# A new order for the mixer of a two-layer hybrid decoder trunk, with a new beginning and a new end

## Chip, cores and metric

One core of one Trainium2 chip runs the whole program. The metric is the device time of one execution in microseconds (us); of a kernel the median over several executions counts, and lower is better.

## What is computed

Two layers over 512 tokens of width 1024, everything in float32. In a layer, `x` goes through a SwiGLU half-step, a mixer, and a second SwiGLU half-step:

```python
x = x + 0.5 * swiglu(rms_norm(x, norm_ffn1[l]), ffn1_w_gate[l], ffn1_w_up[l], ffn1_w_down[l])
x = x + hybrid_mixer(rms_norm(x, norm_mix[l]), w_in[l], w_proj_dil[l], w_proj_sb[l], w_out[l], cos, sin)
x = x + 0.5 * swiglu(rms_norm(x, norm_ffn2[l]), ffn2_w_gate[l], ffn2_w_up[l], ffn2_w_down[l])
...
return rms_norm(x, norm_final)
```

The mixer projects its input to queries, keys and values of 16 heads and to two gates of width 1024. Twelve heads form three groups of dilated window attention (with partial rotary, merged over groups by their softmax denominators). Four heads do stick-breaking attention, whose weights for a query are `exp(log_beta + after)`, where `after` is a running sum of `log_sigmoid(-z)` from the right. Then

```python
y = gate_dil * (o_dil @ w_proj_dil) + gate_sb * (o_sb @ w_proj_sb)
return y @ w_out
```

## The kernel before

Activations lie transposed, features on the 128 partitions and 512 tokens along the free axis, as eight tiles `x0` to `x7`. A float32 product is made of three TensorE matmuls on values split into a rounded high part and a remainder (`mm3`, lines 142 to 144). All weights come from one long array in the order in which they are used, in chunks of eight 128x128 blocks. `Weights.fill` loads a chunk and splits a quarter (four blocks, 128x512) at a time: ScalarE casts `whi` (line 76), VectorE subtracts to get `wlo` (line 77). It runs two quarters ahead of use. Whatever order the projections have in the code must be the order in which `_pack_layer` packs the blocks.

`Norm` scales `x` by the gain and splits it (`scale`, lines 173 to 181), sums squares (`square`), and `finish` turns the sum into a reciprocal root per token, as a row `rb` copied from PSUM to SBUF (line 236). In the first half-step squares and scales of the eight tiles are made up front; `feed` does both for a tile as soon as the stage before has written it. `finale` makes the last two blocks of the last half-step by halves of the tokens and multiplies the result by `rb` (line 295) before it is stored.

The mixer runs in this order of code: both V halves (eight banks of PSUM between them, lines 340 to 376), with `norm.finish` after the first weight quarter; then for each of two pairs of stick-breaking heads `qk_pair`, scores and values together (`stick`, lines 447 to 483); then for each of two dilated head sets `s` the rotary `qk_pair`s and scores, with gates in between as `GATES` says (`dil_scores`), the softmax (`dil_softmax`) and the values (`dil_values`); then the sigmoid gates with the two output projections (`apply_gate`, lines 654 to 660), with one gate pair (d = 7) still to be projected, and `w_out`. A stick-breaking score tile takes Abs, Exp and Ln on ScalarE, an add, a reversed scan (line 464) and a subtraction on VectorE, and an Exp on ScalarE.

PSUM banks go by letter: `m`, `t`, `s`, `o`, two buffers each. The code's order is not the engines' order: the framework's scheduler plays the program on a model of the engines and lets later work go ahead of waiting work, within the banks and buffers that are free; each engine then runs its list strictly in that fixed order.

Of the kernel before, what the change touches and what calls it, by code (L numbers as in the profile page):

```python
# [41 lines left out]

class Weights:
# [4 lines left out]
    def __init__(self, nc, raw, split, hold, w):  # L50
        self.nc, self.raw, self.split, self.hold, self.w = nc, raw, split, hold, w
        self.nq = w.shape[0] * (CB // QB)
        self.pos = 0
        self.ready = {}
        self.done = 0
        self.chunk = None

    def fill(self, q):
        nc = self.nc
        while self.done <= q and self.done < self.nq:  # L60
            c, part = divmod(self.done, CB // QB)
            if part == 0:
                self.chunk = self.raw.tile([P, CB * P], F32, name="wraw", tag="wraw")
                step = P if c == 0 else CB * P
                for o in range(0, CB * P, step * QB):
                    e = min(o + step * QB, CB * P)
                    nc.sync.dma_start(self.chunk[:, o:e], self.w[c, :, o:e])
# [8 lines left out]
            nc.scalar.copy(hi, src)  # L76
# [29 lines left out]
def trunk(ctx, tc, xin, win, gains, rope, masks, out, depth):  # L106
# [16 lines left out]

    nc.scalar.preload_act_table_set(SIGM)
    gain = const.tile([P, gains.shape[1]], F32, name="gain")
    nc.sync.dma_start(gain, gains)
    weights = Weights(nc, rawp, splitp, hpool, win)
    xs = []
    for k in range(KD):
# [3 lines left out]
        if k == 0:  # L133
            weights.fill(0)
# [22 lines left out]
    class Norm:  # L157


        def __init__(self, g, table=None):  # L160
# [4 lines left out]
            self.h = [None] * KD  # L165
            self.acc = None
            self.rest = []

        def feed(self, k):
            self.scale(k)  # L170
            self.square(k)

        def scale(self, k):
            x = xs[k]
            gk = gain[:, self.g + k:self.g + k + 1]
            if not self.last:
                hi = hpool.tile([P, T], F32R, name=f"xh{k}", tag=f"xh{k}")
                lo = hpool.tile([P, T], F32R, name=f"xl{k}", tag=f"xl{k}")
                nc.scalar.activation(hi, x, AF.Copy, bias=0.0, scale=gk)
# [36 lines left out]
        def finish(self, j0=0, j1=NT):  # L216
# [20 lines left out]
            self.rt, self.rb = rt, rb  # L237

    def ffn(norm, nxt, first):
        with ExitStack() as st:  # L240
# [6 lines left out]
            for f in range(NF):  # L247
                pg, pu = [bank(b) for b in ("mt", "mt", "oo")[f % 3]]
                project(pg, norm.h)
                project(pu, norm.h)  # L250
                if f == 0:
                    if first:
                        for k in range(KD):
                            norm.square(k)
                    norm.finish_wide(nw, onesr)
# [21 lines left out]
    def finale(st, hs, nxt):  # L277
# [3 lines left out]
        for c0 in range(0, T, HT):  # L281
# [9 lines left out]
            for k in range(0, KD, 2):  # L291
                o = op.tile([P, 2, HT], F32, name="o", tag="o")
                eng = nc.gpsimd if k == 2 else nc.vector
                for i in range(2):
                    eng.tensor_mul(o[:, i], xs[k + i][:, c], nxt.rb[:, :HT])
                nc.sync.dma_start(out[k:k + 2, :, c].rearrange("k p t -> p k t"), o)

    def mixer(norm, nxt):
# [7 lines left out]
        pp = pool(st, "mixp", 8)  # L306
# [33 lines left out]
        pv = []  # L340
        for half in range(2):
            pv.append([bank(b) for b in ("mmtt", "ssoo")[half]])
            for k in range(KD):
                wh, wl = weights.quarter()
                for j in range(NT):
                    c = slice(j * P, (j + 1) * P)
                    ps = pv[half][j]
                    a, b = h[k][0][:, c], h[k][1][:, c]
                    nc.tensor.matmul(ps, a, wh, start=k == 0, stop=False)
                    nc.tensor.matmul(ps, a, wl, start=False, stop=False)  # L350
                    nc.tensor.matmul(ps, b, wh, start=False, stop=k == KD - 1)
                if half == 0 and k == 0:
                    norm.finish()
                    nc.gpsimd.tensor_mul(cr, cr, norm.rb)
                    nc.gpsimd.tensor_mul(sr, sr, norm.rb)

            def split_v(dst, src, sc):
                v = src.rearrange("p (h d) -> p h d", d=HD)
                nc.scalar.activation(dst[:, :, 0, :], v, AF.Copy, bias=0.0, scale=sc)
                nc.vector.scalar_tensor_tensor(dst[:, :, 1, :], v, sc, dst[:, :, 0, :].bitcast(F32),  # L360
                                               ALU.mult, ALU.subtract)

            if half == 0:
                v0, vs = [], []
                for j in range(NT):
                    sc = norm.rt[:, j:j + 1]
                    for lst, nm, off in ((v0, "v0", 0), (vs, "vs", 256)):
                        t = vp.tile([P, 4, 2, HD], F32R, name=f"{nm}_{j}", tag=f"{nm}_{j}")
# [471 lines left out]
```

## Time and profile before

| | |
|---|---|
| median of 3 runs | 2169.5 us (2168.34 to 2170.79) |
| the profiled execution, its own time | 2166.81 us |
| its span, first to last instruction | 2165.0 us |
| TensorE (PE) busy | 2136.6 us, 99% |
| VectorE (DVE) busy | 1209.4 us, 56% |
| ScalarE (ACT) busy | 892.7 us, 41% |
| GpSimd (POOL) busy | 374.4 us, 17% |
| mean granted TensorE clock | 0.996 |

The profile counts a matmul as busy until its modelled end, and matmuls overlap, so a PE that is 99% busy can still issue more slowly than it might. The two mixers lie at 372 to 672 us and 1443 to 1743 us of the span.

### The profile page before, as it was taken

To read this page: it belongs to the slowest core of one execution; us is meant where nothing else is said; L and a number is where in the kernel's file an instruction comes from. 1 tells how busy PE (TensorE), PEld (TensorE's weight loads), DVE (VectorE), ACT (ScalarE), POOL (GpSimd) and SP (SyncE) were. 2 spreads that over 40 slices of the span, in tenths; PEclk is the share of its full clock that TensorE was granted. 3 is DMA by queue.
4 is the path that set the end of the run, shared out by engine and by line. 5 is a ranking of instruction groups with operands and counts; after the bars stand their busy time and mean duration, and the time that the engine had idled before them with its cause. 6 is when DMAs were issued, how large, how long until landed. Compare 5 with 4: busy or idle time off the path is not lost.

```text
span 2165.0 us, 25866 instructions
## 1 busy us (share of the span) xinstructions
PE 2136.6 (99%) x9772; PEld 1764.2 (81%) x9772; DVE 1209.4 (56%) x1896; ACT 892.7 (41%) x1572; POOL 374.4 (17%) x396
## 2 busy tenths in 40 slices
PE   8999999999999999999999999999999999999998
PEld 7888888878887888888888888888788788888887
DVE  7544433589867655443354444336897666444433
ACT  5333323566564433332333333236664544333332
POOL 2222100021412122210022220000223212222100
PEclk9999999999999999999999999999999999999999
DMA  4333333232224233323233333333222233323222
GB/s 153 97 97 98 102 105 125 88 93 87 79 74 129 96 97 98 97 97 98 88 98 97 98 98 107 108 117 94 87 83 78 79 126 98 98 97 97 97 90 86
DMA packets 64621, 212.80 MB, mean 98 GB/s; under 512 B 7408, under 2 KB 9456, under 8 KB 64496
## 3 DMA queue, kind: packets, MB, share of 16 engines
q1 hardware_dynamic: 63920, 210.10, 30.4%
q8 instruction: 76, 1.25, 0.2%
q10 hardware_dynamic: 576, 1.05, 0.2%
q14 instruction: 49, 0.40, 0.1%
HBM read 200.63 MB, written 6.29 MB: 96 GB/s over the span
## 4 chain that ended last, share of the span: by engine, by line
PE 91%; DVE 5%; issue 2%; ACT 1%; POOL 1%; DMA 0%; SPq 0%; DVEq 0%; POOLq 0%; ACTq 0%
PE ps_o L142 14%; PE ps_o L143 14%; PE ps_o L144 14%; PE ps_m L142 9%; PE ps_m L143 9%; PE ps_m L144 9%; PE ps_t L143 5%; PE ps_t L142 5%; PE ps_t L144 5%; DVE wlo L77 1%; DVE sc L464 1%; PE ps_o L620 0%; POOL bn L554 0%; ACT pt L545 0%; PE ps_s L422 0%
## 5 line engine op out<-in xcount | busy, mean ns | idle before, releaser
L77 DVE TENSOR_TENSOR wlo<-wraw,whi 128x512 fp32r<-128x512 f32 x736 | 593.6, 809 | 584.1 <-ACT whi L76 583.5
L76 ACT CAST whi<-wraw 128x512 fp32r<-128x512 f32 x736 | 454.8, 621 | 963.0 <-PE ps_o L143 486.3
L142 PE MATMUL ps_m<-xh,whi 128*128 128x512 f32 x992 | 390.8, 394 | 8.7 <-ACT whi L76 6.1
L143 PE MATMUL ps_m<-xl,whi 128*128 128x512 f32 x992 | 391.3, 394 | 0.0
L144 PE MATMUL ps_m<-xh,wlo 128*128 128x512 f32 x992 | 390.4, 394 | 0.5 <-DVE wlo L77 0.5
L142 PE MATMUL ps_o<-fh,whi 128*128 128x512 f32 (+1 forms) x748 | 285.9, 382 | 0.0
L143 PE MATMUL ps_o<-fl,whi 128*128 128x512 f32 (+1 forms) x748 | 285.8, 382 | 0.0
L144 PE MATMUL ps_o<-fh,wlo 128*128 128x512 f32 (+1 forms) x748 | 285.8, 382 | 0.0
L260 POOL TENSOR_TENSOR fg<-fg,fs 128x512 f32<-128x512 f32 x88 | 116.4, 1325 | 867.0 <-ACT fs L259 867.0
L142 PEld LDWEIGHTS ps_m<-xh,whi 128*128 128x128 f32 x992 | 187.6, 189 | 49.2 <-ACT whi L76 7.0
L144 PEld LDWEIGHTS ps_m<-xh,wlo 128*128 128x128 f32 x992 | 187.6, 189 | 39.4 <-DVE wlo L77 2.0
L143 PEld LDWEIGHTS ps_m<-xl,whi 128*128 128x128 f32 x992 | 187.7, 189 | 37.9 <-DVE xl L180 0.8
L144 PE MATMUL ps_t<-xh,wlo 128*128 128x512 f32 x480 | 187.0, 390 | 0.0
L142 PE MATMUL ps_t<-xh,whi 128*128 128x512 f32 x480 | 187.0, 390 | 0.0
L143 PE MATMUL ps_t<-xl,whi 128*128 128x512 f32 x480 | 187.0, 390 | 0.0
L143 PE MATMUL ps_o<-xl,whi 128*128 128x512 f32 x448 | 174.5, 390 | 0.0
L142 PE MATMUL ps_o<-xh,whi 128*128 128x512 f32 x448 | 174.5, 390 | 0.0
L144 PE MATMUL ps_o<-xh,wlo 128*128 128x512 f32 x448 | 174.5, 390 | 0.0
L142 PEld LDWEIGHTS ps_o<-fh,whi 128*128 128x128 f32 x748 | 140.6, 188 | 30.1
L143 PEld LDWEIGHTS ps_o<-fl,whi 128*128 128x128 f32 x748 | 140.6, 188 | 30.0
L144 PEld LDWEIGHTS ps_o<-fh,wlo 128*128 128x128 f32 x748 | 140.6, 188 | 30.0
L261 POOL TENSOR_TENSOR fg<-fg,rb 128x512 f32<-128x512 f32 x88 | 116.3, 1324 | 6.3
(218 smaller groups left out, 2706.6 us busy)
## 6 DMA issues: line engine op xcount, KB each, us to landing
wraw<-in_w_dram SPq DMA_DIRECT2D x367, 512.0 KB, 3.5
spill<-x SPq DMA_DIRECT2D x16, 256.0 KB, 2.1
kh<-kh SPq DMA_DIRECT2D x32, 128.0 KB, 2.7
x<-spill SPq DMA_DIRECT2D x16, 256.0 KB, 3.5
x<-in_x_dram SPq DMA_DIRECT2D x8, 256.0 KB, 4.7
out_dram<-o SPq DMA_DIRECT2D x8, 256.0 KB, 2.2
wraw<-in_w_dram SPq DMA_DIRECT2D x2, 256.0 KB, 3.5
cr<-in_rope_dram ACTq DMA_DIRECT2D x2, 256.0 KB, 2.8
```

Of the source, the lines that this page charges most:

```text
L76: nc.scalar.copy(hi, src)
L77: nc.vector.tensor_sub(lo, src, hi.bitcast(F32))
L142: nc.tensor.matmul(ps, w[0], v[0], start=start, stop=False, skip_group_check=True)
L143: nc.tensor.matmul(ps, w[0], v[1], start=False, stop=False, skip_group_check=True)
L144: nc.tensor.matmul(ps, w[1], v[0], start=False, stop=stop, skip_group_check=True)
L260: nc.gpsimd.tensor_mul(g, g, s)
L261: nc.gpsimd.tensor_mul(g, g, norm.rb)
L464: nc.vector.tensor_tensor_scan(cv[:, ::-1], av[:, ::-1], ones[:, 0:1].to_broadcast([P, w]), 0.0, ALU.add, ALU.mult)
```

## The change

The mixer's stick-breaking queries, keys and scores of both pairs come first (`stick_scores`), and their values later (`stick_values`). Between them stand the first V half, the gate pair d = 0, the second V half and the gate pair d = 1. V uses four banks (`t`, `t`, `o`, `o`) for each half. The rotary projection of the first dilated heads is moved out of `dil_scores`, and the values of head set 0 come after the first rotary projection of head set 1. `GATES` puts d = 2, 3 into set 1 and d = 4 to 7 at its end, so that no gate is left for the closing loop. `norm.finish` comes after the first query projection. The ten score buffers are shared out anew, and two outputs use the buffers of `vs`.

At the beginning, seven matmuls on a zeroed tile run before the first real one, x and weight transfers alternate on SP's queue, the gain's transfer goes to ACT's queue, the first cast of weights is done by VectorE, the first gate and up projections are interleaved by k, and squares come after all scales. At the end, three of the four products of a half read the reciprocal root from PSUM. `feed` squares before it scales for the last two tiles.

```diff
-GATES = {(0, 0): (), (0, 1): (0, 1), (0, 2): (), (0, 3): (2,), (1, 0): (3,), (1, 1): (), (1, 2): (), (1, 3): (4, 5, 6)}
+WARM = 7
+GATES = {(0, 0): (), (0, 1): (), (0, 2): (), (0, 3): (), (1, 0): (2, 3), (1, 1): (), (1, 2): (), (1, 3): (4, 5, 6, 7)}
+OTAGS = {"os0": ("os0h", "os0l"), "os1": ("os1h", "os1l"), "od0": ("vs_0", "vs_1"), "od1": ("vs_2", "vs_3")}
...
+    def load(self, eng):
+        c, part = divmod(len(self.early), CB // QB)
+        if part == 0:
+            self.chunk = self.raw.tile([P, CB * P], F32, name="wraw", tag="wraw")
+        o = part * QB * P
+        eng.dma_start(self.chunk[:, o:o + QB * P], self.w[c, :, o:o + QB * P])
+        self.early.append(self.chunk)
...
-            nc.scalar.copy(hi, src)
+            if self.done:
+                nc.scalar.copy(hi, src)
+            else:
+                nc.vector.tensor_copy(hi, src)
...
+    warm = hpool.tile([P, T], F32R, name="warm", tag=f"xh{KD - 1}")
+    nc.vector.memset(warm.bitcast(F32), 0.0)
+    nc.scalar.dma_start(gain, gains)
     nc.scalar.preload_act_table_set(SIGM)
-    nc.sync.dma_start(gain, gains)
...
         nc.sync.dma_start(t, xin[k])
         xs.append(t)
-        if k == 0:
-            weights.fill(0)
+        if k % 2 == 0:
+            weights.load(nc.sync)
+    ps = bank("o")
+    for i in range(WARM):
+        nc.tensor.matmul(ps, warm[:, 0:P], warm, start=True, stop=True, skip_group_check=True)
...
         def feed(self, k):
-            self.scale(k)
-            self.square(k)
+            if k < KD - 2:
+                self.scale(k)
+                self.square(k)
+            else:
+                self.square(k)
+                self.scale(k)
...
-                project(pg, norm.h)
-                project(pu, norm.h)
-                if f == 0:
-                    if first:
+                if first and f == 0:
+                    for k in range(KD):
+                        if k + 4 < KD:
+                            norm.scale(k + 4)
+                        for ps in (pg, pu):
+                            mm3(ps, weights.block(), norm.h[k], k == 0, k == KD - 1)
+                    with tc.issue_after(norm.cast.ins):
                         for k in range(KD):
                             norm.square(k)
+                else:
+                    project(pg, norm.h)
+                    project(pu, norm.h)
...
-                eng = nc.gpsimd if k == 2 else nc.vector
+                eng, r = (nc.gpsimd, nxt.rb) if k == 2 else (nc.vector, nxt.pb)
                 for i in range(2):
-                    eng.tensor_mul(o[:, i], xs[k + i][:, c], nxt.rb[:, :HT])
+                    eng.tensor_mul(o[:, i], xs[k + i][:, c], r[:, :HT])
...
-        pp = pool(st, "mixp", 8)
+        pp = pool(st, "mixp", 10)
...
-            pv.append([bank(b) for b in ("mmtt", "ssoo")[half]])
+        def project_v(half):
+            pv = [bank(b) for b in "ttoo"]
...
-        def qk_pair(kind, view_q, view_k):
+        def qk_pair(kind, view_q, view_k, tag="m"):
             res = []
             for which in ("q", "k"):
-                ps = bank("m")
+                ps = bank(tag if which == "q" else "m")
                 project(ps, h)
+                if norm.rb is None:
+                    norm.finish()
+                    nc.gpsimd.tensor_mul(cr, cr, norm.rb)
+                    nc.gpsimd.tensor_mul(sr, sr, norm.rb)
...
+        def stick_scores(qk):
+            half = pp.tile([P, T], F32, name="sw", tag="pp")
+            heads = []
             for e in range(2):
+                full = [pp.tile([P, T], F32, name="sw", tag="pp") for _ in range(2)]
...
+                    a = (full[0][:, 0:P], half[:, 256 * e:256 * e + 256], full[0][:, P:T], full[1][:, :])[j]
...
-                g = mp.tile([P, T], F32, name="gate", tag="gate", bufs=6)
+                g = mp.tile([P, T], F32, name="gate", tag="gate", bufs=8)
...
-        qs0 = qk_pair("plain", same, to_t)
-        os_.append(stick(0, qs0))
-        qs1 = qk_pair("plain", same, to_t)
-        os_.append(stick(1, qs1))
+        sw = []
+        for p in range(2):
+            sw.append(stick_scores(qk_pair("plain", same, to_t, "mo"[p])))
+        project_v(0)
+        gates[0] = (gate(0, 0), gate(0, 1))
+        project_v(1)
+        gates[1] = (gate(1, 0), gate(1, 1))
+        for p in range(2):
+            os_.append(stick_values(p, sw[p]))
+        qk0 = qk_pair("rope", same, same)
         od = []
+        held = None
         for s in range(2):
+            if s:
+                qk0 = qk_pair("rope", same, same)
+            if held:
+                od.append(dil_values(0, *held))
             tl = dil_tiles()
-            dil_scores(s, *tl)
+            dil_scores(s, qk0, *tl)
             dil_softmax(*tl)
-            od.append(dil_values(s, tl[2], tl[3]))
-            fill(s, 3)
+            held = tl[2], tl[3]
+        od.append(dil_values(1, *held))
+        fill(1, 3)
```

The packing of the weights (`_pack_layer`) follows the new order. The number of real matmuls does not change.

## Rows read from the trace of the kernel before

**Rows 1.** The page: busy time, share of the span and instructions by engine.
```profile
PE 2136.6 (99%) x9772; PEld 1764.2 (81%) x9772; DVE 1209.4 (56%) x1896; ACT 892.7 (41%) x1572; POOL 374.4 (17%) x396
```

**Rows 2.** Timeline of PE, second V half: start, duration; 96 matmuls between these.
```profile
395.72 0.39 PE L349 MATMUL ps_s<-whi,xh 128*128 128x512 f32 x1
...
417.48 0.39 PE L142 MATMUL ps_m<-xh,whi 128*128 128x512 f32 x1
```

**Rows 3.** Layer 0's mixer by stretch: length, busy PE, PEld, DVE, ACT, POOL; PEclk, DMA.
```profile
372.00:412.00 40.00, 40.00 (x185) 33.37 (x185) 17.00 (x30) 15.00 (x27) 4.74 (x6) 1.00 0.34 112
...
452.00:482.00 30.00, 26.68 (x122) 21.43 (x121) 25.39 (x42) 18.39 (x39) 7.41 (x5) 0.94 0.25 78
...
562.00:592.00 30.00, 28.62 (x141) 23.28 (x140) 29.54 (x63) 12.18 (x22) 12.58 (x23) 0.94 0.24 72
...
642.00:652.00 10.00, 8.70 (x45) 6.56 (x44) 5.71 (x9) 3.04 (x6) 0.21 (x1) 1.00 0.11 46
652.00:672.00 20.00, 20.00 (x88) 16.34 (x87) 19.08 (x23) 11.13 (x17) 9.96 (x7) 1.00 0.60 187
sum 300.00, PE 293.99 PEld 245.53 DVE 234.06 ACT 172.86 POOL 66.85; mean PE 36.75 PEld 30.69 DVE 29.26 ACT 21.61 POOL 8.36
```

**Rows 4.** The same view for the mixer of layer 1.
```profile
1523.00:1553.00 30.00, 25.76 (x124) 20.50 (x123) 25.41 (x41) 18.63 (x40) 7.38 (x6) 1.00 0.25 78
...
1633.00:1663.00 30.00, 28.60 (x149) 23.09 (x149) 29.54 (x63) 11.89 (x21) 12.76 (x23) 1.00 0.23 71
...
1713.00:1723.00 10.00, 8.71 (x44) 6.72 (x42) 5.38 (x8) 3.02 (x5) 0.00 (x0) 0.92 0.12 48
```

**Rows 5.** Timeline: a scan beside GpSimd, the matmul behind it, a scan alone.
```profile
460.07 1.62 POOL L396 TENSOR_TENSOR qa<-qa,qb 128x512 f32<-128x512 f32 x1
...
460.47 2.30 DVE L464 TENSOR_TENSOR_SCAN sc<-sw,ones 128x512 f32<-128x512 f32 x1
...
463.64 0.36 PE L421 MATMUL ps_s<-kh,qh 128*128 128x256 f32 x1 [1.31 <-DVE sc L466]
...
505.04 1.21 DVE L464 TENSOR_TENSOR_SCAN sc<-sw,ones 128x512 f32<-128x512 f32 x1
```

**Rows 6.** Groups of DVE, 372 to 672 us: busy, mean ns of one | idle before.
```profile
L77 DVE TENSOR_TENSOR wlo<-wraw,whi 128x512 fp32r<-128x512 f32 x88 | 73.3, 840 | 34.6 <-ACT whi L76 34.4
...
L464 DVE TENSOR_TENSOR_SCAN sc<-sw,ones 128x128 f32<-128x128 f32 (+3 forms) x16 | 16.9, 1066 | 0.2
L466 DVE TENSOR_TENSOR sc<-ps_s,sc 128x128 f32<-128x128 f32 (+3 forms) x16 | 7.6, 482 | 0.3
L463 DVE SCALAR_TENSOR_TENSOR sw<-ps_s,sw 128x128 f32<-128x128 f32 (+3 forms) x16 | 7.5, 481 | 1.1 <-ACT sw L462 1.1
L675 DVE TENSOR_TENSOR yl<-y,yh 128x512 fp32r<-128x512 f32 x7 | 7.5, 1067 | 0.9 <-ACT yh L674 0.7
L360 DVE SCALAR_TENSOR_TENSOR v<-ps_o,rt,v 32x512 fp32r<-32x512 f32 x8 | 6.0, 749 | 0.3
```

**Rows 7.** Timeline of the beginning.
```profile
4.62 0.61 ACT L187 ACTIVATE acc<-x 128x512 f32<-128x512 f32 x1
...
5.79 0.80 PE L142 MATMUL ps_m<-xh,whi 128*128 128x512 f32 x1 [5.79 <-ACT whi L76]
...
10.23 0.63 PE L144 MATMUL ps_m<-xh,wlo 128*128 128x512 f32 x1
10.65 0.63 PE L142 MATMUL ps_m<-xh,whi 128*128 128x512 f32 x1
...
19.88 0.39 PE L142 MATMUL ps_m<-xh,whi 128*128 128x512 f32 x1
```

**Rows 8.** Timeline of the end.
```profile
2154.41 0.42 DVE L288 SCALAR_TENSOR_TENSOR x<-ps_o,x 128x256 f32<-128x256 f32 x1 [4.07 <-PE ps_o L144]
...
2158.08 0.37 ACT L236 COPY rb<-ps_s 128x256 f32<-128x256 f32 x1 [1.70 <-PE ps_s L233]
2158.48 3.15 DVE L295 TENSOR_TENSOR o<-x,rb 128x256 f32<-128x256 f32 x6 [1.32 <-ACT rb L236]
```

More of the change, by code (lines that the diff above doesn't have):

```diff
@@ L61, in fill @@
             c, part = divmod(self.done, CB // QB)
-            if part == 0:
+            if self.done < len(self.early):
+                self.chunk = self.early[self.done]
+            elif part == 0:
                 self.chunk = self.raw.tile([P, CB * P], F32, name="wraw", tag="wraw")
[L64 to L67, printed above, removed]
+                nc.sync.dma_start(self.chunk, self.w[c])
             src = self.chunk[:, part * QB * P:(part + 1) * QB * P]
@@ L122, in bank @@
         return psum.tile([P, 512], F32, name="ps_" + tag, tag=tag)
+    weights = Weights(nc, rawp, splitp, hpool, win)
+    gain = const.tile([P, gains.shape[1]], F32, name="gain")
+    warm = hpool.tile([P, T], F32R, name="warm", tag=f"xh{KD - 1}")
+    nc.vector.memset(warm.bitcast(F32), 0.0)
+    nc.scalar.dma_start(gain, gains)
     nc.scalar.preload_act_table_set(SIGM)
-    gain = const.tile([P, gains.shape[1]], F32, name="gain")
-    nc.sync.dma_start(gain, gains)
-    weights = Weights(nc, rawp, splitp, hpool, win)
     xs = []
@@ L337, in mixer, with split_v @@
         nc.scalar.dma_start(sr, rope[1])
-        pv = []
-        for half in range(2):
-            pv.append([bank(b) for b in ("mmtt", "ssoo")[half]])
+        v0, vs = [], []
+        v12 = vp.tile([P, 4, 8, 2, HD], F32R, name="v12", tag="v12")
+        def split_v(dst, src, sc):
+            v = src.rearrange("p (h d) -> p h d", d=HD)
+            nc.scalar.activation(dst[:, :, 0, :], v, AF.Copy, bias=0.0, scale=sc)
+            nc.vector.scalar_tensor_tensor(dst[:, :, 1, :], v, sc, dst[:, :, 0, :].bitcast(F32),
+                                           ALU.mult, ALU.subtract)
+        def project_v(half):
+            pv = [bank(b) for b in "ttoo"]
             for k in range(KD):
@@ L470, in stick, with stick_values @@
                     ws.append(a)
+                heads.append(ws)
+            return heads
+        def stick_values(p, heads):
+            of = work("of")
+            for e, ws in enumerate(heads):
+                hd = 2 * p + e
                 po = bank("o")
@@ L483, in stick, with gate @@
             return split_o(of, f"os{p}")
-        def gate(d, b):
-            ps = bank("m")
+        def gate(d, b, tag="m"):
+            ps = bank(tag)
             project(ps, h)
@@ L691, in trunk @@
     norm = Norm(0, SIGM)
-    for k in range(KD):
+    for k in range(4):
+        if k % 2 == 0:
+            weights.fill(k // 2)
         norm.scale(k)
-        if k == 3:
-            weights.fill(1)
     mask = const.tile([P, 640], F32, name="mask")
@@ L764, in ffn @@
         gu = np.stack([g, u], 1).reshape(-1, P, P)
+        if l == 0 and first:
+            gu[:2 * KD] = gu[:2 * KD].reshape(2, KD, P, P).transpose(1, 0, 2, 3).reshape(-1, P, P).copy()
         dn = a[dn][l].reshape(NF, P, KD, P).transpose(2, 0, 1, 3).reshape(-1, P, P)
@@ L793, in _pack_layer @@
     pb = a["w_proj_sb"][l].reshape(2, P, KD, P).transpose(2, 0, 1, 3)
-    early = [d for ds in GATES.values() for d in ds]
+    early = [0, 1] + [d for ds in GATES.values() for d in ds]
     mix += [pb[d] for d in sorted(early)]
```

73 lines of the change are left out of this document (30 added, 43 removed).

## The prediction

> **What bounds the kernel now.** I read the page first, for busy time by engine. TensorE is busy 99% of the span and the next engine, VectorE, 56% [rows 1], so this is a kernel in which TensorE issues nearly always, and only time in which it issues too slowly can be won. The timeline gives its full pace: from the first matmul of the second V half to the one after the 96th, 21.76 us pass [rows 2], so 0.227 us each, and 5.44 us for a projection of 24.
>
> Next I asked for busy time by stretch in each mixer, to see where this pace is missed. A stretch loses what PE lacks of its length, and, where the clock column is under 1, that share of its length. In layer 0 the stick-breaking stretch (452 to 482 us) loses 3.32 + 0.06 x 30 = 5.1 us, the stretch of the first dilated softmax (562 to 592) 1.38 + 1.8 = 3.2, the closing loop's start (642 to 652) 1.3 [rows 3]. Layer 1 loses 4.24, 1.4 and 1.29 + 0.8 = 2.1 in the same places [rows 4]. Over both layers: stick-breaking 9.3, softmax 4.6, closing loop 3.4, together 17.3 us. It is slightly too little, since a matmul counts as busy for 0.39 us and its follower could start after 0.23 [rows 2], but it is where the mixer's gain must come from.
>
> The last view is the timeline around one such stop. The matmul of a score tile waits 1.31 us for VectorE's subtraction, which frees the bank; the subtraction stands behind a scan that took 2.30 us while GpSimd multiplied rotary queries, and the same scan alone took 1.21 [rows 5]. So VectorE is late, and partly because GpSimd runs beside it. Its load is uneven: in the first 40 us of the mixer, the V halves, it works 17.0 us, in 452 to 482 it works 25.4 of 30, in 562 to 592 29.5 of 30; over the whole 300 us 234 [rows 3].
>
> **The sum is made against the profiled execution**, 2166.8 us with a span of 2165.0; the median shown is 2169.5, 2.7 us above it, and I add these 2.7 at the end. A difference of about 0.2%, 4.3 us, is what a measurement of this kernel can tell from no change.
>
> **Stick-breaking scores first, V and gates beside them.** No matmul is added or dropped in the mixer. Four projections (21.8 us of PE) now come first, then two V halves and four gates (2 x 21.76 + 4 x 5.44 = 65.3 us) with the score matmuls among them. VectorE's work beside these 65.3 us: 24 weight quarters at 0.84 = 20.2; the sixteen 32-row pieces of V at 0.75 = 12.0; eight half-width pieces of V, bounded by the same 0.75 at 6; four gates, by the same, at 3; sixteen score tiles 16.9 + 7.6 + 7.5 = 32.0 [rows 6]. That is 73, against 65.3 and the score matmuls: VectorE is full, but the 23 us that it now idles in the mixer's first 40 are used, and GpSimd has no rotary work there, so the long scans fall from 2.30 towards 1.21 and the 0.84 of a quarter is an upper end. Nothing but the values waits for the scores, and they come after all of it. I keep 1.3 of the 9.3 us: minus 8.0. The ends: minus 9.3, and, by the slower rival below, plus 22.7.
>
> **V in `t`, `t`, `o`, `o` twice.** The second half waits until the first is evacuated, 8 pieces on VectorE, at most 6 us. The first gate pair, 10.9 us of PE in the `m` banks, hides it. Without that cover it would cost up to 6 us a layer; behind the second half stands the second gate pair, with 12 us of VectorE work against 10.9, so the values may find a `t` bank late by about 1 us. I put 0.5 for both layers together; the ends are 0 and 2 x 6.
>
> **Queries first after the first half-step.** A V half asked for one tile of `x` every 2.7 us; a query projection asks for the eighth at its 22nd matmul, 4.8 us after the half-step's last. Until then that tile needs an add, the square now put ahead (0.61 [rows 7]), a cast and a subtraction, bounded by 0.84 each [rows 6]: 3.1 us. It is hidden; if other VectorE work stood ahead the wait would be about 1 to 2 us a layer. The norm's chain is hidden behind four projections that ask only for banks. On SP the first keys' copies now stand closer behind the eight spill stores and among weight loads, in the order that they had; a load behind such a copy waits for ScalarE's cast of the key, as before. I cost these at nothing, with 0 and 4 us as the ends.
>
> **Values of set 0 held back, gates moved.** The softmax of set 0 now has the next rotary projections (10.9 us) ahead of its values and two gate pairs (21.8) after, instead of one pair. Of 4.6 us I keep 1.6: minus 3.0; the ends are minus 4.6 and 0. What the stretch lacks is VectorE (29.5 of 30), and rotary work is the part that GpSimd slows, which is why some stays.
>
> **No gate in the closing loop.** Before, the last gate pair's 10.9 us lay between the eight output products, and even so VectorE worked 19.1 of 20 us there [rows 3]. Now the pair lies ahead, beside the second softmax; the loop's remainder subtractions (1.07 each, beside GpSimd's adds [rows 6]) have less PE work around them, but the `os` products can still come between. Plus 1.0; the ends are minus 3.4 and 2 x 4.1, half of the pair's 10.9 uncovered less the 1.3 lost now.
>
> **The beginning.** PE starts at 5.79, when ScalarE's cast of weights is done, which stood behind a square (4.62, 0.61). Ten matmuls until 11.08 run at half clock, 0.42 from start to start; the 49th starts at 19.88 [rows 7]. Now VectorE makes that cast, the squares go behind, and x0 is first on its queue. I take the first real matmul at 4.8. Seven dummies at 0.42 take 2.9 us, between about 1.3 and 4.3, before it. The clock rose 5.3 us after the first matmul; the same from 1.3 on leaves four real ones at half clock, 0.8 lost. Interleaving by k asks for a tile of x per six matmuls instead of three; I leave 1 us for late transfers. So 48 matmuls end at 4.8 + 10.9 + 1.8 = 17.5 instead of 19.9: minus 2.4. The ends are 0 (transfers set the pace as now) and minus 4.2 (none late, no cold ones).
>
> **The end.** Six products took 3.15 us beside GpSimd, after a copy of 0.37 that started 0.40 before them [rows 8]. Read from PSUM they start 0.40 earlier and take about 0.42 each, as the residual add from PSUM did: 2.5. Minus 0.4 and minus 0.6, together 1.0; GpSimd's pair ends earlier than VectorE's. The ends are 0, if the stores set the end, and minus 1.2. The Trainium skill speaks against this edit: "VectorE: DVE Perf Modes", Rules for kernel authors, advises to copy PSUM to SBUF first for many operations on a matmul's output; by it this term would be 0 or worse. Against it stands "SBUF — State Buffer", Who interferes with whom: a VectorE instruction with two SBUF inputs contends with a GpSimd instruction that reads SBUF, one with at most one does not. The scan at 2.30 and 1.21 agrees [rows 5].
>
> **The sum.** Mixers: minus 8.0 + 0.5 - 3.0 + 1.0 = minus 9.5. With 2.4 and 1.0: minus 12.9. 2166.8 - 12.9 = 2153.9, and 2.7 more: **2156.6 us**, with 2150 to 2163 as this case's own range.
>
> **Rivals.** *VectorE's waits move instead of going.* It has 234 us to do whatever the order; from the scores on it is now nearly full without a pause, and each stop removed comes back near the rotary work. The mixers gain nothing: 2166.8 - 3.4 + 2.7 = 2166.1. For it speaks the 73 against 65.3; against it, that VectorE is idle 23 us where this work goes, and that stretches at 95% now lose nothing (652 to 672 [rows 3]).
>
> *Slower: score tiles stop TensorE.* VectorE runs its list in order, and weight quarters stand behind score steps that wait for ScalarE. If a tile's add is late, `wlo` is late, and PE waits within two quarters. One stop is 1.31 us [rows 5], and layer 0 lost 5.1 for 3.3 idle through the clock, so 2.0. At every second tile, 16 in both layers, the stretch loses 32 instead of 9.3: plus 22.7 against minus 4.9 of the other terms, 2187.3. It decides from 14.2 us on, seven stops in 32 tiles. Today's 9.3 are like four or five; the longest is tied to GpSimd, which speaks against it.
>
> *Everything goes.* All 17.3 us, 4.2 at the beginning, 1.0 at the end: 2147. The full VectorE speaks against it.
>
> **Chances.** Forecast 0.57, waits move 0.20, slower 0.13, everything 0.10. The second is cut by the 0.2% line (2165.2): 0.07 faster, 0.12 same, 0.01 slower. Slower is then 0.14 with the third; faster 0.57 + 0.10 + 0.07 = 0.74; same 0.12. The range, 2146 to 2171, leaves out most of the slower case and a little below.
>
> **What would show it.** Right: the mixer's stretches with stick scores at clock 1.00 with PE full, long scans near 1.2 us, no PE wait on the subtraction (now L466); first real matmul before 5 us; the last products at 0.42. Wrong: PE waits for `whi`, `wlo` or a `t` bank beside V and the gates, VectorE at 10 of 10 there with PE short, or a longer stop in the closing loop. The prediction fails by most if the fixed order, made on a model, has VectorE late where the weights are split.

## The result and the profile after

The median is 2154.9 us (2154.8 to 2155.5), against 2169.5 us of before in the same runs; the ratio is 0.9936, with a 95% interval of 0.9925 to 0.9948. The profiled execution took 2155.2 us, its span 2153.0.

By the starts of their first matmuls in the two traces the parts compare so: up to the first mixer 372.07 before and 369.00 now (-3.1), mixer of layer 0 345.01 and 341.16 (-3.9), mixer of layer 1 346.15 and 341.24 (-4.9), half-steps the same within 0.1, from the first matmul of the last norm to the end 10.8 and 10.6 (-0.2). Together -12.0, the whole difference of the spans. A mixer here reaches to its last matmul of `w_out`; before, it lay at 372 to 717 us, so that 372 to 672 [rows 3] is not all of it.

The page's busy line of the changed kernel, beside [rows 1]:

```profile
PE 2133.7 (99%) x9779; PEld 1759.8 (82%) x9779; DVE 1213.5 (56%) x1898; ACT 895.8 (42%) x1571; POOL 374.0 (17%) x396
```

Busy time by stretch, columns as in [rows 3]. Most of the scores lie in 408 to 473 (their first matmul is at 394), the stick-breaking values in 473 to 538, the transposes behind the first softmax in 538 to 578, the closing loop's start in 650 to 662; the last three rows are layer 1:

```profile
408.00:473.00 65.00, 65.00 (x304) 54.13 (x303) 50.36 (x84) 49.30 (x93) 0.00 (x0) 1.00 0.25 81
473.00:538.00 65.00, 61.24 (x309) 49.41 (x308) 60.65 (x115) 34.52 (x76) 25.68 (x16) 1.00 0.28 87
538.00:578.00 40.00, 40.00 (x220) 34.40 (x218) 29.65 (x77) 20.85 (x55) 12.33 (x36) 1.00 0.24 73
...
650.00:662.00 12.00, 11.42 (x50) 8.88 (x49) 10.90 (x16) 4.76 (x8) 4.96 (x4) 1.00 0.16 51
...
1541.00:1606.00 65.00, 61.28 (x309) 49.48 (x308) 60.65 (x115) 34.51 (x77) 25.68 (x16) 1.00 0.29 88
1606.00:1646.00 40.00, 40.00 (x223) 34.48 (x222) 29.51 (x76) 20.30 (x53) 13.05 (x36) 1.00 0.24 77
1718.00:1730.00 12.00, 11.42 (x49) 8.94 (x49) 11.05 (x16) 4.11 (x7) 5.71 (x4) 1.00 0.20 62
```

TensorE no longer misses anything beside the scores and the softmax. It misses 3.76 and 3.72 us beside the values, and there GpSimd works 25.7 us on rotary tiles. Before, most of the values lay in a stretch without loss, with less GpSimd work beside them in more time:

```profile
482.00:562.00 80.00, 80.00 (x408) 68.06 (x407) 68.33 (x136) 51.37 (x116) 19.76 (x26) 1.00 0.27 85
```

TensorE's waits in the changed kernel, grouped (total, times, longest):

```profile
PE ps_o L522 <- DVE ptl L463: 7.2, 12, 1.0
...
PE ps_t L164 <- DVE gate L712: 1.2, 2, 0.6
```

`ptl` is the low half of transposed stick weights. One of these stops on the timeline:

```profile
492.10 1.29 POOL L427 TENSOR_TENSOR qb<-qb,sr 128x512 f32<-128x512 f32 x1 [3.60 <-DVE qb L426]
492.43 1.50 DVE L94 TENSOR_TENSOR wlo<-wraw,whi 128x512 fp32r<-128x512 f32 x1
493.47 1.59 POOL L428 TENSOR_TENSOR qa<-qa,qb 128x512 f32<-128x512 f32 x1
494.46 0.54 DVE L463 TENSOR_TENSOR ptl<-ps_t,pth 128x384 fp32r<-128x384 f32 x1
494.93 0.69 DVE L94 TENSOR_TENSOR wlo<-wraw,whi 128x512 fp32r<-128x512 f32 x1
495.06 0.44 PE L522 MATMUL ps_o<-ptl,vs 128*128 128x384 f32 x1 [1.00 <-DVE ptl L463]
```

A subtraction of weights took 1.50 us beside GpSimd's rotary pair, the next one, as the pair ended, 0.69; `ptl` stood behind the long one, and TensorE stood still for 1.00 us. This is the pattern of [rows 5]; now the values wait in place of the scores.

The beginning: seven dummies, then real matmuls at full pace from the second on; the 49th is the last row ([rows 7] has 5.79 and 19.88).

```profile
1.45 3.35 PE L156 MATMUL ps_o<-warm 128*128 128x512 f32 x7 [1.45 <-DVE ones L161]
4.91 0.70 PE L164 MATMUL ps_m<-xh,whi 128*128 128x512 f32 x1
5.45 0.39 PE L164 MATMUL ps_t<-xh,whi 128*128 128x512 f32 x1
...
16.57 0.39 PE L164 MATMUL ps_m<-xh,whi 128*128 128x512 f32 x1
```

The end:

```profile
2142.62 0.42 DVE L323 SCALAR_TENSOR_TENSOR x<-ps_o,x 128x256 f32<-128x256 f32 x1 [5.18 <-PE ps_o L166]
2145.52 1.16 PE L260 MATMUL ps_s<-ident,rt 128*128 128x128 f32 x4 [1.36 <-DVE rt L257]
2146.77 0.37 ACT L263 COPY rb<-ps_s 128x256 f32<-128x256 f32 x1 [2.18 <-PE ps_s L260]
2147.17 2.07 DVE L330 TENSOR_TENSOR o<-x,ps_s 128x256 f32<-128x256 f32 x6 [1.80 <-ACT rb L263]
```

The six products take 2.07 in place of 3.15 [rows 8], but they still start after ScalarE's copy: the wait names it, though they do not read what it writes. Both read the same PSUM tile, and without the copy the wait is gone (run 8). From the copy to the end of the span it is 6.24 us now and was 6.94. From the residual add to the copy it is 4.15 and was 3.67: the four broadcast matmuls took 1.16, and 0.68 before.

### The profile page after: what moved, and what is told of

Its sections match the earlier page's. It is cut to its first block, busy times and chain, and to the rows that moved or that the text cites. A ratio compares the mean times of both kernels' runs of the same rounds, so it can differ in the third digit from the quotient of the medians.

```text
span 2153.0 us, 25941 instructions
## 1 busy us (share of the span) xinstructions
PE 2133.7 (99%) x9779; PEld 1759.8 (82%) x9779; DVE 1213.5 (56%) x1898; ACT 895.8 (42%) x1571; POOL 374.0 (17%) x396
## 4 chain that ended last, share of the span: by engine, by line
PE 90%; DVE 6%; ACT 1%; POOL 1%; issue 1%; DMA 1%; SPq 0%; DVEq 0%; POOLq 0%; ACTq 0%
PE ps_o L164 14%; PE ps_o L165 14%; PE ps_o L166 14%; PE ps_m L165 9%; PE ps_m L164 9%; PE ps_m L166 9%; PE ps_t L164 5%; PE ps_t L165 5%; PE ps_t L166 5%; DVE wlo L94 1%; ACT v L380 1%; PE ps_t L393 1%; PE ps_t L392 1%; PE ps_t L391 1%; PE ps_o L392 1%
## 5 line engine op out<-in xcount | busy, mean ns | idle before, releaser
L94 DVE TENSOR_TENSOR wlo<-wraw,whi 128x512 fp32r<-128x512 f32 x736 | 600.0, 818 | 549.9 <-ACT whi L91 547.1
L164 PE MATMUL ps_m<-xh,whi 128*128 128x512 f32 x976 | 382.9, 392 | 0.2
L165 PE MATMUL ps_m<-xl,whi 128*128 128x512 f32 x976 | 382.3, 392 | 0.0
L166 PE MATMUL ps_m<-xh,wlo 128*128 128x512 f32 x976 | 381.9, 391 | 0.0
L165 PEld LDWEIGHTS ps_m<-xl,whi 128*128 128x128 f32 x976 | 183.3, 188 | 36.2
L164 PE MATMUL ps_o<-xh,whi 128*128 128x512 f32 x464 | 180.7, 389 | 0.0
L166 PE MATMUL ps_o<-xh,wlo 128*128 128x512 f32 x464 | 180.5, 389 | 0.0
L165 PE MATMUL ps_o<-xl,whi 128*128 128x512 f32 x464 | 180.5, 389 | 0.0
```

Source lines behind the costliest of these rows:

```text
L94: nc.vector.tensor_sub(lo, src, hi.bitcast(F32))
L164: nc.tensor.matmul(ps, w[0], v[0], start=start, stop=False, skip_group_check=True)
L165: nc.tensor.matmul(ps, w[0], v[1], start=False, stop=False, skip_group_check=True)
L166: nc.tensor.matmul(ps, w[1], v[0], start=False, stop=stop, skip_group_check=True)
```

## The experiments

**Theory G** after the first look at this profile: the stops beside the values come from GpSimd's rotary multiply and add, which lengthen VectorE's instructions with two SBUF inputs. **Theory L**: VectorE has too much to do after the scores, whoever computes the rotary part. **Theory C**: the values' own chain of transpose, cast and subtraction is longer than the work laid between. In runs 11 and 12 L stands for another rival: that the move to VectorE won because the rotary result came earlier, or because the lists of instructions came out differently.

**1. Rotary multiply and add on VectorE** (on the changed kernel):

```diff
-                    nc.gpsimd.tensor_mul(b, b, sr)
-                    nc.gpsimd.tensor_add(a, a, b)
+                    nc.vector.tensor_mul(b, b, sr)
+                    nc.vector.tensor_add(a, a, b)
```

> Changed kernel with the rotary multiply and add on VectorE instead of GpSimd, nothing left out. In the changed kernel TensorE waits 7.2 us over both layers for the remainder subtraction of the stick-breaking values (ptl). Theory G (VectorE instructions with two SBUF inputs stand still while GpSimd reads SBUF for the rotary work): the weight-quarter subtractions fall to about 0.69 us each, VectorE's busy time in a mixer stays within 5 us of the 233 before although it has 24 more instructions of 0.69, the wait falls to 1 to 4 us, and the time is 2148 to 2155. Theory L (VectorE has too much work there, wherever GpSimd is): the wait grows to over 10 us and the time is 2158 to 2170. Theory C (the values' own chain of transpose, cast, subtraction and two banks is longer than the projections laid between): wait 6 to 8, time 2154 to 2156.

2140.2 us (2139.3 to 2141.6), ratio 0.9869 (0.9855 to 0.9882): more than G expected. Both mixers take 333.8 us. Stretches of values and softmax:

```profile
473.00:538.00 65.00, 64.92 (x337) 55.10 (x336) 62.71 (x140) 39.15 (x89) 1.01 (x6) 1.00 0.33 97
538.00:578.00 40.00, 40.00 (x222) 34.56 (x221) 33.87 (x83) 19.86 (x48) 6.17 (x27) 1.00 0.26 80
```

Beside the values VectorE runs 140 instructions in place of 115 in only 2.1 us more, and TensorE lacks 0.08. Over the span VectorE is busy 1205.9 us, less than 1213.5, with 48 instructions more. L, with a wait over 10 us, is out, and so is C, with one of 6 to 8: no wait for `ptl` is left. But the engines' lists change in places too, so this run alone does not settle contention against order. Run 12 shows that contention alone, without another order, costs time; how the 14.7 us of this run divide between the two is not shown.

**2. Sine half left out**: neither engine multiplies or adds.

```diff
-                    nc.gpsimd.tensor_mul(b, b, sr)
-                    nc.gpsimd.tensor_add(a, a, b)
```

> Changed kernel with the sine half of the rotary embedding left out (GpSimd's multiply and add of each rotary projection; the cosine product and the shuffle stay), so the output is not the reference's. Theory G: the wait for ptl falls from 7.2 us to under 1.5 and the time to 2145 to 2149. Theory C: the wait stays at 6 to 8 and the time at 2153 to 2155. Theory L: VectorE's list is as long as before, the wait stays over 5 and the time over 2151.

2140.4 us (2139.5 to 2140.8), under the 2145 of G, no wait for `ptl`: the same time as with the work on VectorE. On VectorE it costs nothing here; on GpSimd some 14.5 us.

**3. Gate pairs 2 and 3 ahead of the first rotary projection**:

```diff
-GATES = {(0, 0): (), (0, 1): (), (0, 2): (), (0, 3): (), (1, 0): (2, 3), (1, 1): (), (1, 2): (), (1, 3): (4, 5, 6, 7)}
+GATES = {(0, 0): (), (0, 1): (), (0, 2): (), (0, 3): (), (1, 0): (), (1, 1): (), (1, 2): (), (1, 3): (4, 5, 6, 7)}
...
         for p in range(2):
             os_.append(stick_values(p, sw[p]))
+        for d in (2, 3):
+            gates[d] = (gate(d, 0), gate(d, 1))
```

> Changed kernel with the gate pairs 2 and 3 projected right after the gate pair 1, ahead of the first rotary projection, instead of beside the scores of head set 1; weights packed to match. The stick-breaking values then have gates beside them, which give GpSimd nothing to do. Theories G and L: the wait for ptl falls to under 3 us; whether new waits come up beside the first dilated softmax, which loses these gates, is open, 0 to 4 us; time 2150 to 2156. Theory C: the fill is as much as before, wait 6 to 8, time 2155 to 2159.

2157.2 us (2156.4 to 2159.0), ratio 0.9948 (0.9934 to 0.9961): over the 2156 of G and L. Its waits:

```profile
PE ps_m L164 <- DVE qb L426: 2.6, 2, 1.3
PE ps_t L634 <- DVE pt L619: 1.9, 2, 1.0
...
PE ps_o L643 <- DVE ptl L463: 1.3, 1, 1.3
```

The values lose nothing now (65.00 of 65 in 473 to 538), and the softmax stretch has 36.38 of 40. The stops go with the rotary work; G and L, which expected the same here, are not told apart by this run.

**4. The old mixer with the new beginning and end** (old `GATES`, mixer and packing):

> The mixer of the kernel before, with the new beginning, the new end and the new order of squares in feed. If the parts add up as the two traces show them stage by stage (beginning 3.1 us, end 0.2), the time is 2169.5 - 3.3 = 2166.2, between 2165 and 2167.5, the first mixer starts at 369.0 us instead of 372.1, and a mixer takes 345 to 346 us to the end of its output projection. The rival: the feed order alone, or the earlier start, shifts the fixed order so that the mixer changes too; then the time is under 2164 or over 2168.5.

2165.0 us (2162.3 to 2168.7), ratio 0.9983 (0.9974 to 0.9991). By the medians the beginning and the end are worth some 3.5 of the 13 us. But the executions lie far apart, and the profiled one, 2168.0, is near the upper end. In its trace the mixers take 347.8 and 344.7, not 345 to 346, and the first begins at 370.87, not 369.0: the seven dummies ran from 1.46 us as in the changed kernel, but the real matmuls still started 0.42 apart until 9.38, and the 49th at 18.40.

```profile
5.40 0.77 PE L164 MATMUL ps_m<-xh,whi 128*128 128x512 f32 x1 [0.59 <-DVE whi L93]
5.97 0.63 PE L164 MATMUL ps_t<-xh,whi 128*128 128x512 f32 x1
...
9.38 0.54 PE L166 MATMUL ps_m<-xh,wlo 128*128 128x512 f32 x1
9.76 0.39 PE L165 MATMUL ps_t<-xl,whi 128*128 128x512 f32 x1
```

**5. The old kernel with the move of run 1 alone** (its lines 395 and 396, same edit):

> The kernel before, old order, old beginning and end, with only the rotary multiply and add moved from GpSimd to VectorE. If what the reorder won in the mixer (8.8 us over both layers) was won only by keeping VectorE and GpSimd apart, the old order with the move comes to the 2140.2 us of the new order with the move plus the 3.3 us of beginning and end, 2143 to 2146. If the order has a worth of its own (VectorE's idle first 40 us of the mixer used), the old order keeps waits on the score chain and stays at 2148 to 2160. If the move is bad for the old order because VectorE is full there at 452 to 592 us, the time is over 2166.

2177.3 us (2176.1 to 2179.1), ratio 1.0043 (1.0028 to 1.0058): slower. The largest wait, and the stretch that holds it in layer 0:

```profile
PE ps_t L593 <- DVE pt L578: 14.8, 2, 7.4
```
```profile
622.00:632.00 10.00, 3.24 (x18) 2.46 (x17) 3.40 (x18) 5.41 (x19) 3.44 (x16) 0.87 0.18 52
632.00:642.00 10.00, 8.80 (x28) 6.92 (x29) 8.14 (x26) 9.51 (x18) 3.44 (x17) 0.62 0.00 0
```

VectorE is not full there, 3.40 of 10, and over 372 to 672 it works 225.7 us against 234.1 [rows 3]. TensorE has nothing left to cover the second softmax: its list came out with the projections earlier, and the granted clock falls to 0.87 and 0.62 there. The stick-breaking stretch gains as in run 1 (28.34 of 30 in 452 to 482, for 26.68). So the move takes VectorE's load down in the old order too, and loses by the hole that the new list has; the reason that I had, a full VectorE, is wrong.

**6. Gate pair 7 back in the closing loop**:

```diff
-GATES = {(0, 0): (), (0, 1): (), (0, 2): (), (0, 3): (), (1, 0): (2, 3), (1, 1): (), (1, 2): (), (1, 3): (4, 5, 6, 7)}
+GATES = {(0, 0): (), (0, 1): (), (0, 2): (), (0, 3): (), (1, 0): (2, 3), (1, 1): (), (1, 2): (), (1, 3): (4, 5, 6)}
```

> Changed kernel with the gate pair d = 7 back in the closing loop. The prediction's term (the pair's absence from the loop costs 1 us over both layers): time 2153 to 2154.5. Rival: the pair is worth more beside the second softmax and values, and the loop waits for the remainder of the second dilated output again as in the kernel before (1.3 us idle a layer): 2155.5 to 2159.

2157.1 us (2157.0 to 2159.6), 2.2 us slower than the changed kernel. Its mixers are 1.4 and 1.3 us longer. In place of the waits on `gate` (1.2) stands mainly one on the split of the last head's output, as in the kernel before:

```profile
PE ps_t L164 <- ACT od1h L476: 2.6, 2, 1.3
```

The two traces show why. In run 6 the products with `os` of the first seven gates have run by 637; the split starts at 643.3, TensorE waits 1.29 for it, and the gate pair 7 stands behind that wait. In the changed kernel the pair is projected earlier, products with `os` are left over, and they fill TensorE beside the split (650.6) until 653.6, when the first product with `od1h` finds it done.

**7. No dummies**:

```diff
-WARM = 7
+WARM = 0
```

> Changed kernel without the seven matmuls on zeros. If they are what makes the first real matmuls run at full clock, about ten run at half clock again, 0.42 instead of 0.23 each: the 49th real matmul starts 1.5 to 2.5 us later than in the changed kernel (18.1 to 19.1 instead of 16.6) and the time is 2156.2 to 2157.5. Rival: the transfers set the pace at the beginning and the dummies give nothing: the 49th starts at 16.5 to 17.2, time unchanged within 0.7.

2158.1 us (2157.7 to 2158.3), 3.2 us slower.

```profile
5.59 0.76 PE L164 MATMUL ps_m<-xh,whi 128*128 128x512 f32 x1 [5.59 <-DVE whi L93]
6.16 0.63 PE L164 MATMUL ps_t<-xh,whi 128*128 128x512 f32 x1
...
9.57 0.53 PE L166 MATMUL ps_m<-xh,wlo 128*128 128x512 f32 x1
9.94 0.40 PE L165 MATMUL ps_t<-xl,whi 128*128 128x512 f32 x1
...
18.56 0.39 PE L164 MATMUL ps_m<-xh,whi 128*128 128x512 f32 x1
```

Without them the starts of the first ten real matmuls lie 0.42 apart, nearly twice the 0.23 of full pace, and the 49th comes at 18.56, 2.0 later. The trace's first record of the full clock, 2.4 GHz, is at 9.85 us, in the changed kernel's at 5.40. The rest is mainly one wait of 1.6 us on `fg` in the first half-step, which the changed kernel does not have.

**8. Run 1, and all eight end products on VectorE from PSUM without the copy**:

```diff
-            rb = npool.tile([P, T], F32, name="rb", tag="rb", bufs=2)
-            nc.scalar.copy(rb[:, :n * P], pb[:, :n * P])
+            rb = None
+            if not self.last:
+                rb = npool.tile([P, T], F32, name="rb", tag="rb", bufs=2)
+                nc.scalar.copy(rb[:, :n * P], pb[:, :n * P])
...
-                eng, r = (nc.gpsimd, nxt.rb) if k == 2 else (nc.vector, nxt.pb)
+                eng, r = nc.vector, nxt.pb
```

> The changed kernel with the rotary work on VectorE and, at the end, all eight products of each half on VectorE from PSUM, without the copy of the reciprocal root to SBUF. Theory: in the changed kernel the first product starts 0.49 us after the last broadcast matmul because it waits for ScalarE's copy out of the same bank; without the copy it starts within 0.1 us, the first store goes out 0.4 us earlier, and from the last broadcast matmul's end to the end of the span it takes 5.9 us instead of 6.3. Rival: the wait has another cause, and eight products instead of six end later: 6.3 to 7.0 us. The time: 2139.5 to 2140.5.

2139.6 us (2138.6 to 2141.6), not to be told from run 1 by time. The trace shows the end itself:

```profile
2130.76 0.68 PE L260 MATMUL ps_s<-ident,rt 128*128 128x128 f32 x4 [1.36 <-DVE rt L257]
2131.48 2.74 DVE L332 TENSOR_TENSOR o<-x,ps_s 128x256 f32<-128x256 f32 x8 [0.87 <-PE ps_s L260]
```

The first product starts 0.04 after the last broadcast matmul (0.49 in the changed kernel), and from that matmul to the end of the span (2137.2) it is 5.8 us, against 6.3.

**9. Both V halves together, gate pairs behind them**:

```diff
         project_v(0)
+        project_v(1)
         gates[0] = (gate(0, 0), gate(0, 1))
-        project_v(1)
```

> The changed kernel with the two V halves one directly after the other and both gate pairs behind them (the packed weights follow). This takes away the cover under which the first half's four banks are emptied. The prediction said that without that cover the second half waits up to 6 us a layer: up to 2167 by it, and 2156 to 2167 as the range if ScalarE and VectorE empty the banks one after the other and the second half starts with the first bank. Rival: the second half can start on the first bank at once and its 3 matmuls per bank keep TensorE busy while the others are emptied, so 2155 to 2156 and no wait on ps_t or ps_o of the V matmuls over 1 us.

2149.8 us (2149.4 to 2150.0), ratio 0.9915 (0.9902 to 0.9929): 5.1 us faster than the changed kernel, which neither side expected. No V matmul waits, so the cover was not needed. The wait for `ptl` and two stretches of layer 0:

```profile
PE ps_o L522 <- DVE ptl L463: 0.7, 2, 0.4
```
```profile
408.00:473.00 65.00, 65.00 (x309) 54.29 (x307) 53.58 (x90) 51.15 (x97) 0.00 (x0) 1.00 0.29 89
473.00:538.00 65.00, 64.02 (x322) 52.87 (x321) 58.60 (x112) 32.89 (x69) 24.98 (x16) 1.00 0.28 84
```

VectorE does 3.2 us more before the values and 2.1 less beside them: the emptying of the second half's banks is out of the way before GpSimd starts. That this is what saves the 5 us is read from these rows; no run isolates it.

**10. Run 8, and the closing loop's sum on VectorE**:

```diff
-            nc.gpsimd.tensor_add(y, ga, gb)
+            nc.vector.tensor_add(y, ga, gb)
```

> The fastest version so far (rotary multiply and add, and all end products, on VectorE: 2139.6 us) with the sum of the two gated outputs in the closing loop (8 additions of 128x512 a layer) on VectorE too. By theory G alone the additions cost VectorE 0.69 us each and save it the stretching of the instructions beside them, so about nothing in VectorE's time, and the sum is ready about 0.6 us earlier: 2137.5 to 2140. Rival: VectorE is full in that loop (11.7 of 12 us busy) and eight more instructions of 0.69 us make it the bound: 2140 to 2150, with TensorE waiting on the gated product or on yl.

2139.3 us (2139.1 to 2139.8): as G expected, not to be told from run 8. These two are the fastest kernels measured here.

**11. Run 1 with unused GpSimd work beside it**:

```diff
+                    idle = wk.tile([P, 120], F32, name="idle", tag="idle", bufs=1)
+                    for i in range(16):
+                        nc.gpsimd.tensor_mul(idle, cr[:, :120], sr[:, :120])
+                        nc.gpsimd.tensor_add(idle, idle, cr[:, 120:240])
```

> The kernel with the rotary multiply and add on VectorE (2140.2 us), and beside it GpSimd work that nothing uses: for each of the 12 rotary tiles of a mixer 32 multiplications and additions of 128x120 from SBUF. They have no data of the other engines to wait for, so GpSimd starts them once the tables are scaled (about 380 us in layer 0) and works on them beside the scores and values of the stick-breaking part. The lists of VectorE, ScalarE and the DMA queue are the same as without it, TensorE's differ only in where the last dilated values of layer 1 stand among projections. Theory G (what cost the time was GpSimd's reading of SBUF beside VectorE, whatever GpSimd computes): VectorE's wlo rises from 685 ns to 800 or more and the scans from 822 to 950 or more in that stretch, TensorE waits on VectorE there again, and the time is 2146 to 2170. Rival L (the rotary move won because the rotary result came earlier through a shorter chain, or because the instruction lists came out differently): wlo within 5% of 685, no new wait, 2138.5 to 2143.

2237.9 us (2235.9 to 2238.4), far over both. Most of it is not contention: the burst ran on past the softmax, whose small copies stand behind it on GpSimd, and TensorE waited 27.4 us for it in one piece in each layer. Up to there, in 385 to 520, `wlo` takes 779 ns and the scans 946, for 685 and 822 in run 1: longer than L allows, a little short of G's figures. VectorE's and ScalarE's lists also came out different in places. So the burst had to be shorter.

**12. The same with 9 pairs**:

```diff
-                    for i in range(16):
+                    for i in range(9):
```

> The kernel before it with 9 pairs of idle GpSimd instructions for each rotary tile in place of 16. At the 1.37 us a pair that the longer burst showed, 108 pairs end about 148 us after they start at 389, at 537 in layer 0, about when GpSimd's own copies for the softmax are first wanted (536.8 without the burst). The lists of TensorE, VectorE, ScalarE and the DMA queue are the same as with the rotary multiply and add on VectorE and no idle work (2140.2 us), so nothing but the work beside VectorE differs. Theory G: the stick-breaking values lose about 2.5 us a layer as in the longer burst, wlo is 10 to 20% longer there, and the time is 2143 to 2148. Rival L: 2139 to 2141.5, and the longer burst's stops in the values came from its late copies.

2156.3 us (2155.4 to 2158.2), ratio 0.9945 (0.9932 to 0.9959). In the two traces every other engine has the same instructions in the same order, and it is 16.1 us slower than run 1. GpSimd's burst ends in time, at 540.1 in layer 0; its copies for the softmax start after a wait of 4.74 us for data:

```profile
544.87 4.06 POOL L599 COPY bn<-stb 32x4 f32<-32x4 f32 x16 [4.74 <-ACT pt L594]
```

Busy time by stretch, and three groups of VectorE in 385 to 535 (total, mean ns of one), first here and then in run 1:

```profile
408.00:473.00 65.00, 64.88 (x301) 53.69 (x300) 52.24 (x84) 49.33 (x93) 57.16 (x101) 1.00 0.24 82
473.00:538.00 65.00, 62.57 (x315) 51.20 (x315) 64.25 (x124) 33.09 (x71) 58.02 (x90) 1.00 0.26 85
538.00:578.00 40.00, 37.94 (x205) 32.11 (x204) 32.57 (x91) 19.21 (x45) 8.98 (x37) 1.00 0.28 88
```
```profile
L94 DVE TENSOR_TENSOR wlo<-wraw,whi 128x512 fp32r<-128x512 f32 x44 | 34.1, 774 | 12.8 <-ACT whi L91 12.5
L503 DVE TENSOR_TENSOR_SCAN sc<-sw,ones 128x128 f32<-128x128 f32 (+3 forms) x16 | 15.1, 944 | 0.3
L505 DVE TENSOR_TENSOR sc<-ps_s,sc 128x128 f32<-128x128 f32 (+3 forms) x16 | 7.7, 484 | 0.2
```
```profile
L94 DVE TENSOR_TENSOR wlo<-wraw,whi 128x512 fp32r<-128x512 f32 x46 | 31.5, 685 | 14.4 <-ACT whi L91 14.1
L499 DVE TENSOR_TENSOR_SCAN sc<-sw,ones 128x128 f32<-128x128 f32 (+3 forms) x16 | 13.1, 822 | 0.3
L501 DVE TENSOR_TENSOR sc<-ps_s,sc 128x128 f32<-128x128 f32 (+3 forms) x16 | 7.8, 486 | 0.2
```

The first two groups read both operands from SBUF and got longer; the third reads one from PSUM and kept its time.

The values lose 2.4 us, as G said; another 2.1 follow in the next stretch, when the burst is over but VectorE is behind. The mixer is 341.4 us, against 333.8: more than these 4.6 us, since matmuls overlap in the records and shorter gaps do not show as idle. With equal lists the delay can be read matmul by matmul: 0.3 us at run 1's 408, 0.8 at 473, 6.8 at 538 and 8.0 from 560 on. So the values lose 6.0. G holds in kind, its 2143 to 2148 was too small; L's 2139 to 2141.5 is refuted. The burst keeps GpSimd busy for 58.0 us beside the values, the rotary work for 25.7, so the 16.1 us show the mechanism and not its size in the changed kernel.

## Why the prediction was right, and where its steps were not

The time came out 1.7 us under the forecast and on its mechanism in outline: VectorE's idle time beside V and the gates took up the scores, and the softmax and the beginning gained. The sum of the mixers was -9.5 and is -8.8. The parts are less good than the sum, and that they add up so nearly is luck: stick-breaking gave 6.2 us less than said, softmax and closing loop together 4.8 more.

- **Stick-breaking, -8.0: the mis-sized term.** The scores behave as said: no stop, clock 1.00, TensorE full, GpSimd still in 408 to 473, three of the four long scans of a layer at 1.22. (The fourth, at 478.7 beside the first rotary work, took 2.31.) VectorE is not full there, as 73 against 65.3 had it, but works 50.4 of 65; it is nearly full beside the values, 60.65. But by the measure that gave 9.3 before, 7.5 us are lost beside the values (3.76 + 3.72), so the term is -1.8. The rival that waits move instead of going was right for this part. The step that failed is "nothing but the values waits for the scores, and they come after all of it": the values want transposed weights split by the same VectorE, and they now stand beside the first rotary work. I had the price in hand, a scan of 2.30 beside GpSimd and 1.21 alone [rows 5], and used it only for the place that GpSimd left, not for the place to which the work went.
- **V banks and their cover, +0.5.** No wait on a V bank is seen, with the gate pair between the halves or without (run 9). No cover was needed there, and the gates' place costs 5.1 us.
- **Softmax, -3.0.** Both stretches are full now: -4.6. The prediction credited it to the holding back of values and the moved gates. No run takes back either alone, so which of them, or the new order around, did it stays open. (In run 3, without the pairs 2 and 3 there, the stretch has 36.38 of 40, but its rotary work moved too.)
- **Closing loop, +1.0: wrong sign.** It loses 0.6 a layer, 1.2 for 3.4: -2.2. Undoing it costs 2.2 (run 6). The term took the pair for cover that the loop would lose. In the loop it stands behind the wait that it should cover; placed ahead, it leaves the products with `os` to cover that wait, which the prediction had only as a possibility.
- **Queries first, 0.** Right: no wait in the mixers' first 40 us.
- **Beginning, -2.4.** Up to the first mixer it is -3.1: matmuls are at full pace from the second real one on, not the fifth. The dummies make most of it (run 7), but not in every execution (run 4).
- **End, -1.0.** It is -0.2. The products are shorter than said (0.345 each, 0.42 expected), but start no earlier, since ScalarE's copy of the same tile goes first, and in this execution the broadcast took 1.16 us (0.68 before, and also in runs 2, 6 and 7, which have the same end). The Trainium skill, "VectorE: DVE Perf Modes", Rules for kernel authors, offers a choice: read PSUM at its rate, or copy to SBUF first for many operations. Here eight products out of PSUM, without the copy and with GpSimd still, took 0.34 each and ended sooner (run 8); products out of SBUF with GpSimd still were not run.
- **The median's offset.** I added 2.7 us for the distance of the profiled execution from the median; after the change the two agree within 0.3. The sum alone, 2153.9, was 1.3 us under the profiled execution's 2155.2.
- **What could be won.** The 17.3 us were called slightly too little. With the stops gone (run 1), the two mixers are 23.6 us shorter than before, so the measure missed over a quarter. And the slower rival's 14.2 us is where the time equals the time before; by the 4.3 us that a measurement can tell, it would need 18.5.

The rival "everything goes" (2147) was taken as unlikely because VectorE was full. Its limit was GpSimd: with the rotary work moved, nearly all stops of the mixers go, and the time is 2139 to 2140 (runs 1, 8 and 10).

## What to carry to other kernels

When work moves to a stretch where the engine that sets the pace runs faster, price the stretch that it leaves for its followers as well: here the scores got rid of GpSimd and the values got it. Before a second engine takes over elementwise work, compare the summed time of the first engine with and without it, since its offered relief can lengthen the first engine's instructions beside it. Ask of independent matmul work put in as cover whether there is a wait, and whether the work stands ahead of it: between the V halves there was none, and in the closing loop the work stood behind.

## What the runs showed of the hardware

- GpSimd's SBUF work alone slows VectorE enough to set the time: unused multiplications and additions of 128x120 made `wlo` 13% longer (685 to 774 ns), the scans 15% (822 to 944 ns), and the kernel 16.1 us slower. A single `wlo` took 1.50 us beside a 128x512 pair and 0.69 as the pair ended. The Trainium skill, "SBUF — State Buffer", Who interferes with whom, has VectorE and GpSimd share a port pair under an exclusive lock. The traces agree that the two interfere; that it is a lock no run here shows.
- VectorE's instructions with one operand in PSUM kept their time beside GpSimd: the subtraction of scores 484 ns beside the burst and 486 without it, the products at the end 0.345 us beside GpSimd's pair and 0.34 with GpSimd still (run 8).
- The seven dummies did not always bring the clock up. Of eleven profiled executions with them, ten have the first record of the full clock at 4.8 to 6.6 us, that of run 4 at 9.7, about as without them (9.9 in run 7). What differed is open.
- Forty-eight more instructions on VectorE left it 7.6 us less busy (1205.9 and 1213.5).
- The granted clock falls to half, 1.2 GHz, in TensorE's waits at the end of all fourteen profiled executions. Where it had fallen by about the start of the four broadcast matmuls, they took 1.16 to 1.19 us (seven executions, the changed kernel's at 0.52 in 2145.5 to 2146.7); where it fell after them, 0.68 (six); in one it fell between, 0.87. Why it comes earlier in some is open.
